# Gate matmuls and selection transposes on another pair of PSUM banks, and 12 expert dot products from one stage to the next

## The chip, the cores and the metric

One Trainium2 chip, one of its cores. The metric is the device time of one execution in microseconds (us). Engines are named as in the profile: PE is the matmul engine (TensorE), PEld its weight loads, which run beside the matmuls, DVE is VectorE, ACT is ScalarE, POOL is GpSimd, SP is the engine that issues the plain DMAs.

## What is computed

A decoder trunk of two layers over 272 tokens (16 meta tokens and 256 of the sequence) of width 1024, all in float32. Each layer first mixes tokens (an RG-LRU group and a latent-attention group) and then adds a PEER block, which this change touches:

```
x += W_out [ norm(RG-LRU group) ; norm(MLA group) ]
h  = RMSNorm(x)
q  = (h @ wq) as (token, 8 heads, 2 halves, 128)
s  = q . subkeys                       # 128 scores for each half
top 16 of each half -> 256 pair sums -> top 16 experts of 128*128, gates = softmax
x += sum over the 8*16 experts:  gate * gelu(h . u[expert]) * v[expert]
```

So for each token 128 of 16384 experts count, and u and v are tables of 16384 rows of 1024 numbers, 64 MB each for one layer.

## The kernel before

**Dense and sparse tokens.** For most tokens (SD = 224 of the 256 in layer 0, 208 in layer 1) a layer is computed densely. The *u stage* runs over 128 blocks j of 128 experts: it loads the block of u (1024 x 128 numbers, 512 KB), multiplies it with all tokens, and puts gelu of the result into the large tile `act` (128 experts x 128 blocks x SD tokens). The *gates* multiply `act` by a matrix that is zero but for the 128 chosen experts of each token. The *v stage* runs over 128 blocks of v and adds v times `act` into four PSUM banks. The other 48 tokens (in layer 0 the 16 meta tokens and 32 more, in layer 1 the last 48) are computed sparsely, in three groups g of 16 tokens: a gather is one indirect DMA, issued by POOL, of 128 rows (16 tokens by 8 heads, the s-th of the 16 picks) from u or v. A gathered u tile gives dot products on DVE (`w = 0`, L1067), a gathered v tile is scaled and added on DVE (`w = 1`, L1069 and L1071). A layer has 3 x 2 x 16 = 96 gathers, and the 32 dots of the groups 0 and 1 may be done early, in the u stage; what is not done there is spread over the v stage.

**One order for all loads.** `order` is written out when the program is made: for each stage its blocks, and between them the gathers. `UB` says how many gathers are put between u blocks: an entry (lo, hi, n) spreads n of them over the blocks lo to hi. Layer 0 has 17 of them, so 79 fall into its v stage; layer 1 has 32, so 64 fall into its v stage, about one every second block (`VEND`). Loads are issued in that order, the plain ones by SP, the gathers by POOL, into a ring of 7 tiles of 512 KB (`raw`), which parts of `act` and `gtab` join when they are free; a load waits until its tile has been read. Loaded tiles are taken in the same order.

**Three matmuls for one.** A block is split into two float16 tiles, hi on ACT (L230) and lo on DVE (L231), in three buffers each (`NHL`), two blocks ahead of PE. A u block is 24 matmuls: 8 x (hi by hi, hi by lo: L256, L257) and 8 of lo (L260); a v block is 24 at L1165.

**Work between the u blocks.** `bgq` is a list of generators, one after another, and `pump`, called once for each u block, advances the first until the costs that it yields have used up a credit. Their order: the top-16 searches (`top_head`), `dense_sel(0)`, `dense_sel(1)`, then `gates`. `dense_sel(t)` picks the experts of 128 tokens on DVE (`select_idx`) and then, for two index tiles and the gate values, transposes on PE into a g bank (L940), which DVE copies to `gtab` (L943, L945, L946). `gates` goes in steps b of 8 tokens (28 in layer 0, 26 in layer 1): one-hot tiles on DVE and ACT (`onehot`, L967 to L974), two banks of 8 matmuls each (`mm`, L983), and then `act` times the bank on DVE for the blocks that are done (L993), and a copy of the bank on ACT for those that are not (L995).

**PSUM.** `ps(tag)` gives the next bank of a tag: u has 2 banks, g has 2, v has 4. Banks of a tag go round, and an instruction that writes one waits until its earlier content has been read. In the u stage the blocks use u; the transposes, the gates, and the row tiles of the sparse tokens (L1038) use g. The v banks hold the query matmuls before the u stage and the four sums of the v stage after it.

The program is ordered for each engine by a planner (Tile) that follows the order of the text, with its own estimate of when an instruction can start; each engine then runs its list in order.

Of the kernel before, what the change touches and what calls it, by code (L numbers as in the profile page):

```python
# [46 lines left out]
WS = 1024.0  # L47
NSP = (32, 48)
NU = (2, 2)
UB = (((64, 127, 16), (116, 124, 1)), ((60, 127, 32),))  # L50
PF = 7
XV = 6
NHL = 3
# [91 lines left out]
def trunk(tc, a, out, dbg=None):  # L145
# [6 lines left out]
    def bc(ap, axis, n):  # L152
        ap = ap.unsqueeze(axis)
        s = list(ap.shape)
        s[axis] = n
        return ap.to_broadcast(s)

    def flat(ap):
        return ap.rearrange("p a b -> p (a b)")

    with ExitStack() as ctx:
# [6 lines left out]
        def ps(tag):  # L168
            return psp.tile([128, 512], F32, name="ps_" + tag, tag=tag, bufs=PB[tag])

        def gathers(l):
            ng = (NM if l == 0 else 0) // 16 + NSP[l] // 16
            r = [(g, w) for g in range(ng) for w in range(2)]
            r = [(g, 0) for g in range(NU[l])] + [x for x in r if x[1] or x[0] >= NU[l]]
            return [(g, w, s) for g, w in r for s in range(16)]

        order = []
        for l in range(L):
# [4 lines left out]
            for b in range(NK):  # L183
                order.append(("uT", l, b))
                want = sum(n * min(max(b - lo, 0) / (hi - lo), 1.0) for lo, hi, n in UB[l])
                while len(gathers(l)) - len(gs) < want:
# [85 lines left out]
        def area(tag, dt, shape=None, name=None):  # L272
            return per.tile(shape or [128, 8, T], dt, name=name or tag, tag=tag)
# [561 lines left out]
        def peer(l, col, hh, hl, rs, wq0):  # L835
            with tc.tile_pool(name="peer", bufs=1) as pp:
# [64 lines left out]
                bgq = []  # L901
                credit = [0.0]

                def pump(budget):
                    credit[0] = min(credit[0] + budget, 2.0)
                    while credit[0] > 0 and bgq:
                        try:
                            credit[0] -= next(bgq[0])
                        except StopIteration:
                            bgq.pop(0)  # L910

# [11 lines left out]
                def dense_sel(t):  # L923
                    r = {}
                    c0 = cur[0]
                    yield from select_idx(al, tv[t], ti[t], 8, GSCALE, r)
                    cur[0] = c0
                    if t == 1 and SD < S:
                        if l:
                            V.tensor_scalar(out=comb[:, 1], in0=flat(r["ix"][:, 1]), scalar1=128.0 * l, scalar2=None, op0=ALU.add)  # L930
                        V.scalar_tensor_tensor(out=comb[:, 0].bitcast(I32), in0=comb[:, 1] if l else flat(r["ix"][:, 1]), scalar=128.0, in1=flat(r["ix"][:, 0]), op0=ALU.mult, op1=ALU.add)
                        A.activation(comb[:, 1], flat(r["ga"]), AF.Copy, scale=1.0 / GSCALE)
                        for g in range(n0g // 16, NG):
                            p = toks[g] - NM - 128
                            ready.add(g)
                            for h in range(8):
                                G.dma_start(out=egs[h * 16:h * 16 + 16, g], in_=comb[p:p + 16, :, h * 16:h * 16 + 16])  # L937
                    for k, srct in enumerate((r["ix"][:, 0], r["ix"][:, 1], r["ga"])):
                        tp = ps("g")
                        P.transpose(tp[:, 0:128], flat(srct), ident)  # L940
                        s = slice(t * 128, t * 128 + 128)
                        if k < 2:
                            V.tensor_copy((i1T, i2T)[k][:, s], bc(tp[:, 0:128], 2, 2))  # L943
                        else:
                            V.tensor_copy(gh[:, s], bc(tp[:, 0:128], 2, 2))  # L945
                            V.tensor_tensor(out=gl[:, s], in0=tp[:, 0:128], in1=gh[:, s, 0], op=ALU.subtract)  # L946
                        yield 0.3
# [4 lines left out]
                def gates():  # L952
                    for e in range(NK * SD + 2 * D + 512, PS - D, D):
                        free.append((st["conv"] - 1, l, flata[:, e:e + D]))
                    oh["a"] = area("gx", F16, [128, 2, 2, 8, 128], "oha")
                    oh["b"] = area("gy", F16, [128, 2, 2, 8, 128], "ohb")
                    NB = SD // 8
                    iob = bc(iota, 1, 8)

                    def pairs(ap):  # L960
                        return ap.rearrange("p t (j e) -> p t j e", e=2)

                    def onehot(b):
                        s = slice(b * 8, b * 8 + 8)
                        oa, oe = oh["a"][:, b % 2, 0], oh["a"][:, b % 2, 1]
                        ob = oh["b"][:, b % 2]
                        V.tensor_tensor(out=pairs(oa), in0=iob, in1=bc(i1T[:, s], 2, 64), op=ALU.is_equal)  # L967
                        yield 0.6
                        V.tensor_tensor(out=pairs(oe), in0=iob, in1=bc(i2T[:, s], 2, 64), op=ALU.is_equal)  # L969
                        yield 0.6  # L970
                        V.tensor_tensor(out=pairs(ob[:, 0]), in0=pairs(oe), in1=bc(gh[:, s], 2, 64), op=ALU.mult)
                        yield 0.6
                        for t in range(8):
                            A.activation(ob[:, 1, t], oe[:, t], AF.Copy, scale=gl[:, b * 8 + t:b * 8 + t + 1])  # L974

                    def mm(b):
                        oa, ob = oh["a"][:, b % 2, 0], oh["b"][:, b % 2]
                        r = []
                        for s in range(2):
                            g = ps("g")  # L980
                            for t in range(4):
                                for k in range(2):
                                    P.matmul(g[:, t * 128:t * 128 + 128], oa[:, s * 4 + t], ob[:, k, s * 4 + t], start=t == 0 and k == 0, stop=t == 3 and k == 1, skip_group_check=True)  # L983
                            r.append(g)
                        return r

                    def mult(b, gs):
                        J = prog["u"]
                        for s, g in enumerate(gs):
                            t0 = b * 8 + s * 4  # L990
                            gv = g.rearrange("p (t j) -> p j t", t=4)
                            av = act[:, 0:J, t0:t0 + 4]
                            V.scalar_tensor_tensor(out=av, in0=av, scalar=1.0 / GSCALE, in1=gv[:, 0:J], op0=ALU.mult, op1=ALU.mult)  # L993
                            if J < NK:
                                A.activation(act[:, J:NK, t0:t0 + 4], gv[:, J:NK], AF.Copy, scale=1.0 / GSCALE)  # L995
                        prog["t"] = (b + 1) * 8
                        yield 0.14 + J * 8 / 960.0

                    for b in range(NB + 1):
                        if b < NB:  # L1000
                            yield from onehot(b)
                        if b:
                            gs = mm(b - 1)
                            yield from mult(b - 1, gs)
# [114 lines left out]
                if l == 0:  # L1119
                    bgq.append(sparse_top())  # L1120
                bgq += [dense_sel(0), dense_sel(1), gates()]
                xh, xlo = hnh[:, :, NM:NM + SD], hnl[:, :, NM:NM + SD]
                gt2 = pp.tile([128, 2, SD], F32, name="gt2")

                for j in range(NK):
                    w = block("uT", l, j)
                    if j % 2 == 0:
                        o2 = ps("u")
                    mm3(o2[:, (j % 2) * SD:(j % 2) * SD + SD], w, xh, xlo, first=j % 2 == 0)
                    if j % 2:  # L1130
                        td = prog["t"]
                        ov = o2[:, 0:2 * SD].rearrange("p (j t) -> p j t", j=2)
                        if td < SD:
                            A.activation(act[:, j - 1:j + 1, td:SD], ov[:, :, td:SD], AF.Gelu, scale=1.0 / WS)  # L1134
                        if td:
                            A.activation(gt2[:, :, 0:td], ov[:, :, 0:td], AF.Gelu, scale=1.0 / WS)  # L1136
                            V.tensor_tensor(out=act[:, j - 1:j + 1, 0:td], in0=act[:, j - 1:j + 1, 0:td], in1=gt2[:, :, 0:td], op=ALU.mult)
                        prog["u"] = j + 1
                    pump(PUMP[1] - prog["t"] / 960.0)
# [91 lines left out]
```

## Time and profile before

| | us |
|---|---|
| median of 3 runs | 1651.68 |
| lowest and highest | 1649.93, 1652.34 |
| the profiled execution | 1654.24 |
| its span, from the first to the last instruction | 1652.5 |
| mean granted clock of PE | 0.991 |

The profile is of one execution. Busy times are of its span; the 1.7 us between span and time lie before the first and after the last instruction. A matmul's end is modelled, so a pause of PE is better read from its weight loads.

### The profile page before, as it was taken

To read this page: it belongs to the slowest core of one execution; us is meant where nothing else is said; L and a number is where in the kernel's file an instruction comes from. 1 tells how busy PE (TensorE), PEld (TensorE's weight loads), DVE (VectorE), ACT (ScalarE), POOL (GpSimd) and SP (SyncE) were. 2 spreads that over 40 slices of the span, in tenths; PEclk is the share of its full clock that TensorE was granted. 3 is DMA by queue.
4 is the path that set the end of the run, shared out by engine and by line. 5 is a ranking of instruction groups with operands and counts; after the bars stand their busy time and mean duration, and the time that the engine had idled before them with its cause. 6 is when DMAs were issued, how large, how long until landed. Compare 5 with 4: busy or idle time off the path is not lost. (4 is left out here: it accounts for less than half of the span.)

```text
span 1652.5 us, 40158 instructions
## 1 busy us (share of the span) xinstructions
PE 1581.6 (96%) x15926; PEld 1474.2 (89%) x15926; DVE 1503.8 (91%) x3074; ACT 1096.1 (66%) x2001; POOL 348.6 (21%) x256
## 2 busy tenths in 40 slices
PE   9999998999998999999999899889998999999998
PEld 6667898999998999999977678779998999999998
DVE  6889999979989999999978889998899999999996
ACT  6857565789886655555557665567988766555554
POOL 1000000101111434544310000002131144743240
PEclk9999999999999999999999999999999999999999
DMA  8304465667777999999963044568678899999993
GB/s 307 115 7 165 140 220 199 219 196 243 243 241 255 343 408 383 353 365 368 339 243 111 31 144 141 179 215 261 205 281 277 274 338 408 395 375 358 370 367 115
DMA packets 117709, 421.22 MB, mean 255 GB/s; under 512 B 14416, under 2 KB 15824, under 8 KB 117008
## 3 DMA queue, kind: packets, MB, share of 16 engines
q1 hardware_dynamic: 88592, 317.88, 53.9%
q0 software_dynamic: 28928, 100.76, 16.7%
q8 instruction: 125, 2.05, 0.5%
q14 instruction: 64, 0.52, 0.1%
HBM read 417.46 MB, written 1.05 MB: 253 GB/s over the span
## 5 line engine op out<-in xcount | busy, mean ns | idle before, releaser
L230 ACT ACTIVATE hi<-raw 128x1024 f16<-128x1024 f32 x450 | 473.3, 1054 | 259.9 <-PE ps_v L1165 114.9
L231 DVE SCALAR_TENSOR_TENSOR lo<-raw,hi 128x1024 f16<-128x1024 f32 x450 | 549.8, 1225 | 53.5 <-ACT hi L230 45.5
L1165 PE MATMUL ps_v<-ww,hi 128*128 128x224 f16 (+1 forms) x4096 | 422.2, 256 | 2.8 <-ACT ww L1146 1.7
L256 PE MATMUL ps_u<-hn,hi 128*128 128x224 f16 (+2 forms) x2112 | 417.2, 258 | 4.8 <-ACT act L1134 3.5
L257 PE MATMUL ps_u<-hn,hi 128*128 128x224 f16 (+2 forms) x2112 | 416.9, 258 | 0.0
L1165 PEld LDWEIGHTS <-hi 128*128 128x128 f16 x4096 | 380.4, 98 | 3.5 <-issue 3.5
L256 PEld LDWEIGHTS <-hi 128*128 128x128 f16 x2656 | 261.6, 98 | 21.4 <-issue 7.9
L257 PEld LDWEIGHTS <-hi 128*128 128x128 f16 x2656 | 261.3, 98 | 19.9 <-issue 8.6
L260 PEld LDWEIGHTS <-lo 128*128 128x128 f16 x2656 | 248.1, 98 | 31.6 <-DVE lo L231 20.7
L260 PE MATMUL ps_u<-hn,lo 128*128 128x224 f16 (+2 forms) x2112 | 242.9, 257 | 13.2 <-DVE lo L231 13.0
L1165 PE MATMUL ps_v<-ww,lo 128*128 128x224 f16 (+1 forms) x2048 | 233.6, 256 | 1.0 <-DVE lo L231 1.0
L230 ACT ACTIVATE hi<-act 128x1024 f16<-128x1024 f32 x122 | 128.9, 1057 | 113.8 <-PE ps_v L1165 93.9
L1165 PEld LDWEIGHTS <-lo 128*128 128x128 f16 x2048 | 190.8, 98 | 1.2 <-DVE lo L231 1.2
L1084 POOL DMA_INDIRECT raw<-ur,act x68 | 97.5, 1434 | 360.5 <-DVE lo L231 206.5
L231 DVE SCALAR_TENSOR_TENSOR lo<-act,hi 128x1024 f16<-128x1024 f32 x122 | 148.9, 1224 | 17.0 <-ACT hi L230 15.7
L937 POOL DMA_DIRECT2D act<-act x40 | 20.3, 518 | 603.5 <-DMA raw<-uT 599.8
L974 ACT ACTIVATE ohb<-oha,gtab 128x128 f16<-128x128 f16 x432 | 137.0, 396 | 13.1 <-DVE oha L969 11.9
L256 PE MATMUL ps_v<-hgx,hi 128*128 128x272 f16 (+1 forms) x480 | 114.4, 278 | 2.7 <-DVE hT L1206 2.5
L257 PE MATMUL ps_v<-hgx,hi 128*128 128x272 f16 (+1 forms) x480 | 114.1, 278 | 0.2 <-DVE hgx L325 0.2
L1084 POOL DMA_INDIRECT raw<-v,act x46 | 79.6, 1731 | 96.9 <-DVE lo L231 79.8
L1084 POOL DMA_INDIRECT act<-v,act x43 | 76.7, 1785 | 89.5 <-DVE lo L231 70.8
L1147 DVE TENSOR_TENSOR ww<-act,ww 128x448 f16<-128x448 f32 (+1 forms) x128 | 77.1, 604 | 0.0
(321 smaller groups left out, 2009.7 us busy)
## 6 DMA issues: line engine op xcount, KB each, us to landing
raw<-uT SPq DMA_DIRECT2D x239, 512.0 KB
raw<-v SPq DMA_DIRECT2D x135, 512.0 KB
act<-v SPq DMA_DIRECT2D x105, 512.0 KB
raw<-wq SPq DMA_DIRECT2D x32, 512.0 KB
raw<-w_in SPq DMA_DIRECT2D x28, 512.0 KB
act<-uT SPq DMA_DIRECT2D x17, 512.0 KB
raw<-w_out SPq DMA_DIRECT2D x16, 512.0 KB
gtab<-v SPq DMA_DIRECT2D x16, 512.0 KB
```

Of the source, the lines that this page charges most:

```text
L230: A.activation(hi, r, AF.Copy, scale=WS)
L231: V.scalar_tensor_tensor(out=lo, in0=r, scalar=WS, in1=hi, op0=ALU.mult, op1=ALU.subtract)
L256: P.matmul(o, hi[:, s], xhi[:, c], start=first and c == 0, stop=False, skip_group_check=True)
L257: P.matmul(o, hi[:, s], xlo[:, c], start=False, stop=False, skip_group_check=True)
L260: P.matmul(o, lo[:, s], xhi[:, c], start=False, stop=c == n - 1, skip_group_check=True)
L937: G.dma_start(out=egs[h * 16:h * 16 + 16, g], in_=comb[p:p + 16, :, h * 16:h * 16 + 16])
L974: A.activation(ob[:, 1, t], oe[:, t], AF.Copy, scale=gl[:, b * 8 + t:b * 8 + t + 1])
L1084: G.indirect_dma_start(out=t, out_offset=None, in_=tab, in_offset=bass.IndirectOffsetOnAxis(ap=ei[g][:, s:s + 1], axis=0))
L1147: V.tensor_tensor(out=ww[:, b, 1], in0=act[:, j:j + 2], in1=ww[:, b, 0], op=ALU.subtract)
L1165: P.matmul(o, (hi, hi, lo)[k][:, s], (wh, wl, wh)[k], start=j == 0 and k == 0 and c % 2 == 0, stop=j == NK - 1 and k == 2, skip_group_chec ...
```

## The change

Four edits. In layer 1, 20 instead of 32 gathers stand between the u blocks 60 to 127, so that 12 dots, and their gathers, fall into the v stage, which then has 76. The three transposes of `dense_sel` and the two banks of a gate step are taken from tag v instead of g. Before its transposes `dense_sel` yields None, at which `pump` stops for this block, so that they come one u block later. NHL stays 3.

```diff
-UB = (((64, 127, 16), (116, 124, 1)), ((60, 127, 32),))
+UB = (((64, 127, 16), (116, 124, 1)), ((60, 127, 20),))
@@ pump
                         try:
-                            credit[0] -= next(bgq[0])
+                            c = next(bgq[0])
+                            if c is None:
+                                break
+                            credit[0] -= c
                         except StopIteration:
@@ dense_sel
+                    yield None
                     for k, srct in enumerate((r["ix"][:, 0], r["ix"][:, 1], r["ga"])):
-                        tp = ps("g")
+                        tp = ps("v")
                         P.transpose(tp[:, 0:128], flat(srct), ident)
@@ gates, mm
                         for s in range(2):
-                            g = ps("g")
+                            g = ps("v")
```

## Rows read from the trace of the kernel before

**Rows 1.** The first part of the page: busy time, share of the span and instructions of each engine.

```profile
PE 1581.6 (96%) x15926; PEld 1474.2 (89%) x15926; DVE 1503.8 (91%) x3074; ACT 1096.1 (66%) x2001; POOL 348.6 (21%) x256
```

**Rows 2.** Waits of the whole span: engine, what waited and at which line, for what, then us in total, times, longest us.

```profile
PEld L983 <- issue: 16.8, 17, 2.5
...
PEld ps_g L940 <- DVE gtab L943: 8.6, 2, 4.7
```

**Rows 3.** PE in order of time, rows around the selection and the gates of both layers: start us, us, line, operation, tiles, shapes, and in brackets the idle time before it and what ended it.

```profile
291.53 0.47 PE L940 MATMUL ps_g<-cst,act 128*128 128x128 f32 x1 [3.69 <-DVE gtab L943]
...
294.78 0.93 PE L260 MATMUL ps_u<-hn,lo 128*128 128x224 f16 x8
...
530.42 1.86 PE L983 MATMUL ps_g<-ohb,oha 128*128 128x128 f16 x16 [2.36 <-ACT act L995]
...
539.00 0.93 PE L260 MATMUL ps_u<-hn,lo 128*128 128x224 f16 x8
...
541.30 0.93 PE L260 MATMUL ps_u<-hn,lo 128*128 128x224 f16 x8
...
1111.12 0.47 PE L940 MATMUL ps_g<-cst,act 128*128 128x128 f32 x1 [4.45 <-DVE gtab L943]
...
1112.61 1.54 PE L260 MATMUL ps_u<-hn,lo 128*128 128x208 f16 x8
...
1280.98 0.82 PE L983 MATMUL ps_g<-ohb,oha 128*128 128x128 f16 x8 [2.06 <-ACT act L995]
```

**Rows 4.** Four short windows: the window and its length in us, busy us (and instructions) of each engine, the granted clock of PE as a share of its full speed, the share of the DMA engines, GB/s.

```profile
291.00:298.00 7.00, 6.47 (x51) 5.84 (x52) 7.00 (x17) 4.68 (x5) 0.00 (x0) 0.76 0.63 212
527.00:540.00 13.00, 10.64 (x103) 10.14 (x101) 10.95 (x15) 5.42 (x12) 2.80 (x3) 0.87 0.76 262
1111.00:1116.00 5.00, 4.88 (x39) 4.43 (x40) 3.96 (x10) 2.91 (x4) 0.00 (x0) 0.70 0.61 210
1280.00:1288.00 8.00, 7.02 (x67) 6.70 (x67) 8.00 (x13) 6.27 (x17) 2.07 (x2) 0.79 0.74 250
```

**Rows 5.** Waits in layer 1's v stage, from 1356 us to 1650, columns as in rows 2.

```profile
POOL act L1084 <- DVE lo L231: 60.6, 18, 11.9
...
DVE acc L1071 <- DMA raw<-v,act: 3.0, 2, 2.5
...
PEld L1165 <- DVE lo L231: 1.2, 1, 1.2
```

**Rows 6.** Windows by stage, columns as in rows 4, in the order PE, PEld, DVE, ACT, POOL: layer 0's gates, to the end of its u stage; layer 1's gates; layer 0's v stage; layer 1's v stage, then a stretch near its end and one around its beginning.

```profile
340.00:542.00 202.00, 195.71 (x2188) 192.75 (x2186) 185.64 (x276) 166.45 (x428) 30.47 (x21) 0.99 0.71 234
...
1186.00:1333.00 147.00, 137.22 (x1601) 133.49 (x1602) 143.96 (x221) 122.38 (x313) 36.51 (x25) 0.99 0.77 268
543.00:845.00 302.00, 300.31 (x3124) 299.88 (x3123) 278.21 (x339) 166.38 (x199) 125.27 (x84) 1.00 0.96 361
1366.00:1646.00 280.00, 278.36 (x3111) 277.96 (x3108) 254.85 (x275) 161.48 (x195) 111.43 (x59) 1.00 0.91 345
...
1620.00:1640.00 20.00, 20.00 (x224) 20.00 (x222) 16.34 (x17) 10.16 (x12) 0.00 (x0) 1.00 0.10 35
...
1356.00:1381.00 25.00, 23.52 (x263) 23.19 (x261) 24.92 (x31) 16.43 (x27) 13.66 (x6) 1.00 1.02 404
```

**Rows 7.** DVE in order of time, lo tiles after the two waits of the transposes: of the eight in layer 0 the first and the last, and two of layer 1.

```profile
288.42 1.23 DVE L231 SCALAR_TENSOR_TENSOR lo<-raw,hi 128x1024 f16<-128x1024 f32 x1
...
307.51 1.23 DVE L231 SCALAR_TENSOR_TENSOR lo<-raw,hi 128x1024 f16<-128x1024 f32 x1
...
1111.98 1.22 DVE L231 SCALAR_TENSOR_TENSOR lo<-raw,hi 128x1024 f16<-128x1024 f32 x1
1114.24 1.23 DVE L231 SCALAR_TENSOR_TENSOR lo<-raw,hi 128x1024 f16<-128x1024 f32 x1 [1.04 <-PE ps_u L260]
```

**Rows 8.** Waits in the gate stretches, columns as in rows 2: PEld in layer 0's (340 to 542), PEld in layer 1's (1186 to 1333), ACT in layer 0's.

```profile
PEld L983 <- issue: 5.4, 5, 2.5
...
PEld L983 <- issue: 11.4, 12, 2.2
...
ACT act L995 <- DVE act L993: 26.6, 18, 5.4
```

**Rows 9.** DVE in order of time in layer 1's gates: one dot and the lo tile after it.

```profile
1217.01 1.23 DVE L1067 SCALAR_TENSOR_TENSOR raw<-raw,act 128x1024 f32<-128x1024 f32 x1
...
1218.15 1.23 DVE L231 SCALAR_TENSOR_TENSOR lo<-raw,hi 128x1024 f16<-128x1024 f32 x1
```

**Rows 10.** Groups of DVE's instructions in layer 1's gates (1186 to 1333): count, busy us, mean ns of one, idle us before them. These are the early dots.

```profile
L1067 DVE SCALAR_TENSOR_TENSOR raw<-raw,act 128x1024 f32<-128x1024 f32 x20 | 24.4, 1222 | 1.9 <-ACT act L1039 1.9
...
L1067 DVE SCALAR_TENSOR_TENSOR act<-act 128x1024 f32<-128x1024 f32 x5 | 6.1, 1223 | 0.0
```

**Rows 11.** The gathers' line on POOL, first in layer 1's gates (1186 to 1333), then in its v stage (1356 to 1646): duration ns min/median/max, first and last start us.

```profile
L1084 POOL DMA_INDIRECT raw<-ur,act x20: 947/1688/1887, 1190.4 to 1327.2; - x20
...
L1084 POOL DMA_INDIRECT raw<-v,act x22: 947/1996/3667, 1360.6 to 1616.2; - x22
```

**Rows 12.** POOL in order of time, early in layer 1's v stage.

```profile
1407.29 3.66 POOL L1084 DMA_INDIRECT act<-v,act  x1 [0.30 <-issue]
1411.26 3.66 POOL L1084 DMA_INDIRECT raw<-v,act  x1 [0.30 <-issue]
```

**Rows 13.** The chain of work that ended last, a piece of it: start us, us, what. It is a gather from its issue to its landing.

```profile
1381.31 8.79 DMA raw<-v,act
```

## The prediction

> **What bounds the kernel now.** I read the page's head and busy line first, then the waits of TensorE, the clock, and the same stretches by engine. [rows 1]: PE is busy for 96% of the span and DVE for 91%, so most of the time is bare matmul time, and only what TensorE stands idle for can be won. [rows 2] names the idle time at the edited lines. Its weight-load rows are the truest, since matmul ends are modelled: 16.8 us in 17 waits before the gate matmuls (L983), and 8.6 us in 2 waits before the third selection transpose (L940), for DVE's copy of an earlier one (L943). [rows 3] shows the longest and what ended them: the transposes at 291.53 and 1111.12, and the gate matmuls at 530.42 and 1280.98, which waited for ACT's read-out of an earlier gate bank (L995). There are two g banks; a gate step takes both, and three transposes want three.
>
> **The clock after a long stop.** In [rows 4] the granted clock is 0.76, 0.87, 0.70 and 0.79 in four short windows, which lie on just these four stops of 2.06 us or more. The lower level is 1.2 GHz, half of the upper 2.4. The full-speed time lost in each is the window times what is missing: 7 x 0.24 = 1.7, 13 x 0.13 = 1.7, 5 x 0.30 = 1.5, 8 x 0.21 = 1.7, together 6.6 us. If the stops go, so do these.
>
> **The ceiling.** 16.8 + 8.6 + 6.6 + 1.2 (one wait for a lo tile early in layer 1's v stage, [rows 5]) = 33.2 us. The edit touches no other TensorE wait.
>
> **What may hold the gain back** is DVE. [rows 6]: in layer 0's gate stretch (340 to 542) DVE is busy 185.6 of 202 us, so 16 are free; in layer 1's (1186 to 1333) 143.96 of 147. There TensorE's waits only mirror a full DVE: take the wait alone away, and TensorE waits next for the lo tiles that DVE makes.
>
> **Part 1, transposes on v banks and a block later.** No instruction is added. With four banks the third transpose no longer needs the first one's copy. The delay takes six transposes and their copies one block back (2.30 us in layer 0 by [rows 3], x 208/224 columns = 2.14 in layer 1), and the gates behind them. Their last matmuls are at 530.42 in layer 0, whose v stage begins at 543, and before 1333 in layer 1, with the v stage from 1366 [rows 3, 6]. Those 12 us or more hide it; past them, each block would cost its 2.3.
> What is late next is a lo. Layer 0: the eight lo tiles after the stop begin between 288.42 and 307.51 [rows 7], and the eighth is ready 1.2 later, at 308.7. Before, the lo matmuls of the first of these blocks began at 294.78 and, at 2.30 a block, those of the eighth at 294.78 + 7 x 2.30 = 310.9. So 2.2 comes back by then unless DVE is relieved too; the ends are 2.2 and 3.7 + 1.7 = 5.4, and I take 2.5, near the row. Layer 1: the lo of 1111.98 is ready at 1113.2 [rows 7], and TensorE reached its block, two after that of 1112.61, at 1112.61 + 2 x 2.14 + 0.6 of half clock (eight lo matmuls took 1.54 there, 0.93 at 541.30 with more columns, [rows 3]) = 1117.5. DVE had caught up by then: at 1114.24 it waited 1.04 for TensorE [rows 7]. So 4.3 comes back (ends 2.2 as in layer 0, and 4.5 + 1.5 = 6.0).
>
> **Part 2, gates on four v banks.** Step b now needs the bank of step b-2, not of b-1. A step takes (530.42 - 340)/27 = 7.1 us in layer 0 [rows 3, 6] and the longest wait was 2.5 [rows 2], so the bank itself should never bind again. The v banks are idle here: the last query matmul is past, and the sums of the v stage want them only after the last gate read-out. Layer 0: 5.4 us of waits [rows 8] + 1.7 of clock = 7.1 at most, 0 at least. ACT stands 26.6 us behind DVE's multiply in this stretch [rows 8], and hi casts queue behind that read-out, so a part turns up again as a late hi or lo; DVE has 16 us free, and I take 5. Layer 1: 11.4 [rows 8] + 1.7 = 13.1 at most, which needs part 3.
>
> **Part 3, 12 dots from u to v.** A dot holds DVE for 1.14 us from its start to the next instruction's ([rows 9], 1217.01 to 1218.15; the accumulator read lies under it). Layer 1's gate stretch holds 20 + 5 = 25 of the 32 dots [rows 10]. 20/32 of them, 15.6, stay, and DVE gets 9.4 x 1.14 = 10.7 us lighter: 133.2. TensorE without its waits needs 147 - 13.1 = 133.9. At the 98% that DVE shows before, it takes 136, a gain of 11; two engines equally full jostle, so 10 (ends 3.0, DVE's idle time with nothing moved, and 13.1).
> In v, 12 x 1.14 = 13.7 us come on top of DVE's 254.9 of 280 [rows 6]: 96%. That costs 0, if all of it falls into the 25 us that DVE idles there, and 13.7 if none does. The nearest row is layer 0's v stage: 79 gathers against the 76 here, DVE at 92%, 361 GB/s, and TensorE's weight loads idle for 2.1 us in all [rows 6]. I take 1.5. The transfers: 12 x 0.524 MB = 6.3 MB more, 15.6 us at the 404 GB/s of full queues at 1356; the engines are all but empty (0.10) in the 20 us from 1620 [rows 6], so it fits. The early wait for a lo [rows 5] came with DVE 3.0 us behind late gathers; DVE enters v less behind, so 1.0 of the 1.2 comes back. On POOL the 12 issues move behind the other early ones, and only DVE's dots wait for them; SP's loads draw on the same buffers, which u gets back and v gives.
> The Trainium skill, "SBUF — State Buffer", section "SBUF: two separate sides", says that the descriptors of POOL-queue DMAs can't be written while DVE runs a two-port fast mode. DVE makes its float16 one-hot tiles in u alone, so by that rule gathers issue faster in v and the moved ones cost nothing: the sum would be 1.5 us better. The trace does not agree: an issue takes 1688 ns in the middle in u and 1996 in v [rows 11].
>
> **Sum.** 2.5 + 4.3 + 5 + 10 + 1.0 - 1.5 = 21.3 us. The profiled execution took 1654.24 us (span 1652.5, 1.7 around it): 1632.9. It lay 2.56 above the median of the runs, so 1630.4; I say **1630 us**.
>
> **Rivals.**
> *The wait moves* (0.22). The gate matmuls run ahead, and TensorE then waits for hi and lo: layer 0's gates give nothing, layer 1's half. For it: DVE at 98%, ACT 26.6 us behind DVE. Against: 12 dots leave. 2.5 + 4.3 + 0 + 5 + 1 - 1.5 = 11.3: 1640.
> *DVE's work is only moved* (0.07), so the change does not do what it is to do. If DVE bounds layer 1 from the selection to the end, its 4.3 is not had, and u's 10.7 comes back as 13.7 in v: 2.5 + 10.7 - 13.7 = -0.5, so 1652, no change that can be measured. For it: DVE's 143.96 of 147 us; against: its 25 idle us in v.
> *Gathers pace layer 1's v stage* (0.07; slower). From 1407 on each issue took 3.67 us on POOL and came 3.97 after the one before [rows 12]. If all 76 ran so, the stage takes 76 x 3.97 + 8.8 for a landing [rows 13] = 311 against 280: 31 lost, 1661. It decides from a spacing of (280 + 21 - 8.8)/76 = 3.85 us. Against: layer 0 brought 79 in 302 us, 3.82 each, and POOL itself mostly waits in v for a tile to be read, 60.6 us for those in act alone [rows 5].
> The skill's "DMA: Bandwidth & Descriptors", section "SWDGE vs HWDGE vs iDMA", says that the software and hardware queues take turns in each DMA engine. Half of 404 GB/s would be 2.6 us a gather, 197 us for 76: by that rule this rival can't decide. At 3.97 us the row gives gathers a third of the rate, less than that.
> *All of it* (0.05). The whole ceiling: 1654.2 - 33.2 - 2.6 = 1618.
>
> **How the numbers follow.** The forecast has 0.59, its own range 1622 to 1638. With *the wait moves*, out to 1645, the range **1620 to 1645** holds 0.81. About 0.2% (3.3 us) is what a measurement here can tell. Faster 0.86 (forecast, moved wait, all of it), same 0.07, slower 0.07.
>
> **What would show it.** Right: no L940 waiting for L943 and no L983 waiting for L995 among TensorE's waits; no clock dip near 290, 530, 1110, 1280; 28 rather than 16 gathers from ur in layer 1's v stage, DVE near 96% there. Wrong: as much new waiting of L256, L257 or L260 in u for hi or lo tiles (the wait moved), or of L1165 for lo tiles while DVE waits for gathers (paced by gathers).

## The result and the profile after

The changed kernel takes **1637.68 us** (median of 4 runs, 1636.75 to 1638.29) against 1651.26 for the kernel before on the same chip: a ratio of 0.9918, 95% interval 0.9900 to 0.9935, so 13.6 us or 0.8% less. The forecast was 1630 with 1620 to 1645. The time lies in the range, and just inside the forecast's own (1622 to 1638), but 7.7 us above the forecast and nearer to the rival *the wait moves* (1640). The profiled execution took 1637.41 us, its span 1635.6. From L908 on, lines of the changed file are three higher, and four from the transposes on: these are L944, the gate matmuls L987, their read-outs L997 and L999, the dots L1071, gathers L1088, the gelu read-out of a u bank L1138, v matmuls L1169.

The first part of the page after, which answers [rows 1] (busy time, share of the span and instructions of each engine):

```profile
PE 1574.9 (96%) x15926; PEld 1469.6 (90%) x15926; DVE 1501.4 (92%) x3073; ACT 1092.9 (67%) x2000; POOL 336.8 (21%) x256
```

The span fell by 16.9 us. TensorE runs the same 15926 matmuls, and DVE is busy for 2.4 us less: what went is idle time, and matmuls at half clock.

Waits of the whole span, the kernel before and then after (engine, what waited, for what, then us in total, times, longest us). Of after there is no row left for the gate matmuls or the third transpose, which made 16.8 and 8.6 us in [rows 2]:

```profile
PEld L260 <- DVE lo L231: 20.7, 31, 1.9
...
PEld L257 <- issue: 8.6, 15, 1.1
...
PEld L256 <- ACT hi L230: 2.1, 4, 0.9
```

```profile
PEld L260 <- DVE lo L231: 28.1, 42, 3.9
...
PEld L257 <- issue: 13.9, 22, 1.8
...
PEld L256 <- ACT hi L230: 7.0, 11, 1.2
```

25.4 us of waits left, and 7.4 + 5.3 + 4.9 = 17.6 us came in at the u blocks' own matmuls, for lo tiles, hi tiles and what stands behind them.

Short windows of after at the places of [rows 4], and a new one, 492 to 502 (window and length, busy us and instructions of PE, PEld, DVE, ACT, POOL, granted clock, DMA share, GB/s):

```profile
286.00:293.00 7.00, 6.15 (x62) 5.48 (x60) 6.93 (x22) 4.68 (x5) 0.00 (x0) 1.00 0.64 213
492.00:502.00 10.00, 6.33 (x56) 5.60 (x54) 7.27 (x11) 4.05 (x11) 2.69 (x2) 0.83 0.50 185
524.00:537.00 13.00, 12.85 (x141) 12.68 (x139) 12.31 (x17) 7.55 (x15) 4.55 (x3) 1.00 0.76 272
1108.00:1113.00 5.00, 5.00 (x59) 5.00 (x57) 5.00 (x9) 4.80 (x7) 0.00 (x0) 1.00 0.65 188
1273.00:1281.00 8.00, 7.44 (x89) 7.09 (x88) 8.00 (x12) 6.06 (x18) 1.69 (x1) 1.00 0.76 274
```

All four dips of the clock are gone, as forecast, and one has come where there was none (before, the clock is 1.00 in 494 to 503, round the same blocks). The stages of [rows 6], after: layer 0's gates, layer 1's gates (1178.6 to 1316.6, between the same blocks as 1186 to 1333 before), layer 0's v stage, layer 1's v stage, same columns:

```profile
340.00:536.00 196.00, 191.86 (x2154) 189.93 (x2152) 180.53 (x269) 162.90 (x419) 25.30 (x20) 0.99 0.70 234
1178.60:1316.60 138.00, 134.82 (x1601) 131.32 (x1600) 133.92 (x202) 118.99 (x310) 21.55 (x15) 1.00 0.74 257
537.00:840.00 303.00, 300.04 (x3123) 299.87 (x3123) 279.52 (x337) 166.46 (x200) 126.18 (x85) 1.00 0.96 363
1352.00:1631.00 279.00, 278.59 (x3114) 278.33 (x3111) 265.32 (x303) 160.11 (x192) 122.93 (x70) 1.00 0.93 363
```

Layer 1's v stage carries 12 more dots (DVE 265 of 279 us, 95%) and TensorE is busy for 278.6 of 279.

Stretches that begin and end at other times are compared by blocks. This table, worked out from the traces, is the time from the first lo matmul (L260) of one u block to that of another, and for the v stage from the end of its first lo matmuls to its last matmul ("to v": from block 127's first lo matmul to that end). The kernels are those of the experiments below. Each column is one execution. Kernels with the same layer 0 (after, e4 and e8; e1 and e9) differ by up to 0.8 us in its u rows and 1.2 in its v stage, so less than that in one row is read only where several kernels repeat it.

```
us                 before  e1    e2    e3    e4    e9    e10  after  e6    e8    e11
L0 u 34-44           29.0  29.1  29.1  28.7  28.7  29.1  28.7  28.7  28.7  28.7  28.5
L0 u 56-100         122.1 120.1 122.5 124.2 120.1 120.1 124.1 120.5 120.1 120.1 120.1
L0 u 100-127         77.2  75.7  77.2  75.7  74.8  75.8  75.5  75.6  70.1  75.6  70.1
L0 to v               5.2   7.0   5.2   5.2   6.9   7.4   5.2   6.9   5.2   7.4   5.2
L0 v                297.6 297.6 297.6 297.6 297.6 298.8 297.6 297.6 300.9 298.8 300.3
L1 u 26-44           46.1  47.6  46.3  43.5  43.5  46.9  43.5  43.5  43.5  43.5  42.9
L1 u 58-112         151.4 151.0 146.9 151.8 151.5 141.3 146.8 142.3 142.3 137.6 141.3
L1 u 112-127         32.1  32.1  32.1  32.1  32.1  32.9  32.1  32.9  32.9  32.1  32.9
L1 v                278.5 278.2 277.3 278.1 278.3 277.3 277.3 277.3 277.3 289.1 277.3
span               1652.5 1650.2 1646.0 1647.9 1644.8 1638.9 1640.0 1635.6 1632.3 1643.0 1628.3
```

### The profile page after: what moved, and what is told of

Read it like the earlier page. It is cut to its first block, busy times and chain, and to the rows that moved or that the text cites. A ratio compares the mean times of both kernels' runs of the same rounds, so it can differ in the third digit from the quotient of the medians.

```text
span 1635.6 us, 40192 instructions
## 1 busy us (share of the span) xinstructions
PE 1574.9 (96%) x15926; PEld 1469.6 (90%) x15926; DVE 1501.4 (92%) x3073; ACT 1092.9 (67%) x2000; POOL 336.8 (21%) x256
## 5 line engine op out<-in xcount | busy, mean ns | idle before, releaser
L230 ACT ACTIVATE hi<-raw 128x1024 f16<-128x1024 f32 x442 | 463.8, 1055 | 236.5 <-PE ps_v L1169 111.9
L231 DVE SCALAR_TENSOR_TENSOR lo<-raw,hi 128x1024 f16<-128x1024 f32 x442 | 536.1, 1217 | 44.0 <-ACT hi L230 40.3
L1169 PE MATMUL ps_v<-ww,hi 128*128 128x224 f16 (+1 forms) x4096 | 422.3, 256 | 4.5 <-DVE ww L1151 2.8
L1169 PEld LDWEIGHTS <-hi 128*128 128x128 f16 x4096 | 380.4, 98 | 5.2 <-issue 5.2
L257 PEld LDWEIGHTS <-hi 128*128 128x128 f16 x2656 | 260.4, 98 | 24.6 <-issue 13.9
L260 PEld LDWEIGHTS <-lo 128*128 128x128 f16 x2656 | 246.5, 98 | 38.7 <-DVE lo L231 28.1
L260 PE MATMUL ps_u<-hn,lo 128*128 128x224 f16 (+2 forms) x2112 | 242.2, 257 | 18.0 <-DVE lo L231 17.5
L1169 PE MATMUL ps_v<-ww,lo 128*128 128x224 f16 (+1 forms) x2048 | 233.5, 256 | 0.0
L1169 PEld LDWEIGHTS <-lo 128*128 128x128 f16 x2048 | 190.9, 98 | 0.0
L1088 POOL DMA_INDIRECT raw<-ur,act x69 | 93.2, 1351 | 374.3 <-DVE lo L231 224.4
L1088 POOL DMA_INDIRECT act<-v,act x44 | 86.5, 1967 | 71.1 <-DVE lo L231 41.1
L1088 POOL DMA_INDIRECT raw<-v,act x49 | 72.9, 1488 | 97.0 <-DVE lo L231 48.6
```

What stands on the lines that cost most here:

```text
L230: A.activation(hi, r, AF.Copy, scale=WS)
L231: V.scalar_tensor_tensor(out=lo, in0=r, scalar=WS, in1=hi, op0=ALU.mult, op1=ALU.subtract)
L257: P.matmul(o, hi[:, s], xlo[:, c], start=False, stop=False, skip_group_check=True)
L260: P.matmul(o, lo[:, s], xhi[:, c], start=False, stop=c == n - 1, skip_group_check=True)
L1088: G.indirect_dma_start(out=t, out_offset=None, in_=tab, in_offset=bass.IndirectOffsetOnAxis(ap=ei[g][:, s:s + 1], axis=0))
L1169: P.matmul(o, (hi, hi, lo)[k][:, s], (wh, wl, wh)[k], start=j == 0 and k == 0 and c % 2 == 0, stop=j == NK - 1 and k == 2, skip_group_chec ...
```

## The experiments

The question was which edit earns what. The theory: in layer 1's gates two limits stand in series, the two g banks and a full DVE, and each hides the other. Its rivals: DVE alone is the limit (the moved dots are all of the gain), or the banks alone are. Kernels of one wave were compared with runs of the kernel before on the same chip, whose medians were 1652.0 (e1 to e4), 1652.4 (e5 to e8) and 1653.66 (e9 to e12).

**e1_gates_v: the banks alone** (on the kernel before)

```diff
                         for s in range(2):
-                            g = ps("g")
+                            g = ps("v")
```

> The kernel before with one edit: the gate banks on tag v. Theory A (two limits in series: in layer 1's gates DVE is full, 143.96 of 147 us, so banks alone give at most its 3 us of idle time there, and about 1.4 in layer 0): about 1647 us, the L983 waits for L995 gone, new waits of L260 for lo tiles in layer 1 of about 8 us. Rival B (only DVE's work counts): 1651, nothing. Rival C (only the banks count): 8.2 in layer 1 and 1.4 in layer 0 as in the changed kernel, 1642.

Measured: 1653.24, ratio 1.0010 [1.0002, 1.0019]. Weight-load waits of layer 1's gates (1180 to 1333), and the stretch as a window:

```profile
PEld L257 <- issue: 3.6, 3, 1.7
PEld L260 <- DVE lo L231: 2.6, 5, 0.6
PEld L983 <- issue: 2.5, 5, 1.6
PEld L256 <- ACT hi L230: 1.4, 2, 0.7
```

```profile
1186.00:1333.00 147.00, 138.30 (x1611) 133.85 (x1610) 145.29 (x222) 122.03 (x309) 38.84 (x26) 0.99 0.77 271
```

The wait for the bank fell from the 11.4 us of [rows 8] to 2.5, and 3.6 + 2.6 + 1.4 us of other waits stand in its place; DVE is busy for 145.3 of 147 us, and the blocks take 151.0 instead of 151.4. More banks alone buy nothing where the engine that reads and feeds them is full. The theory's time, 1647, was missed by 6 us: by the time alone the rival that only DVE's work counts (1651) is nearer, and e9 decides against it. In layer 0, where DVE has idle time, the blocks 56 to 127 win 2.0 + 1.5 us and 1.8 is given back on the way to v. The Trainium skill, "Perfetto Trace Analysis", section "Matmul Optimizations", asks for all 8 PSUM banks to be used; in the u stage this run puts work on the four that lay idle, and it is no faster.

**e2_dots: the dots alone**

```diff
-UB = (((64, 127, 16), (116, 124, 1)), ((60, 127, 32),))
+UB = (((64, 127, 16), (116, 124, 1)), ((60, 127, 20),))
```

> The kernel before with one edit: 20 early dots in layer 1 instead of 32. Theory A: DVE is 10.7 us lighter in layer 1's gates, but the read-outs still hold the two g banks; about half of the 11.4 us of L983 waits goes, and 1 us at the start of v: 1645. Rival B (only DVE's work counts): all of layer 1's 8.2 and the 1.3 of v, 1642. Rival C: only the 1.3 of v, 1650. If the 12 dots cost in v what they hold DVE there (13.7 us), slower than 1651 in B's or C's case.

Measured: 1647.43, ratio 0.9969 [0.9959, 0.9979]. The window of layer 1's gates, and what TensorE waits for there (1180 to 1330):

```profile
1185.00:1327.00 142.00, 135.19 (x1593) 132.61 (x1593) 137.11 (x207) 120.89 (x314) 21.89 (x15) 0.99 0.76 258
```

```profile
PEld L983 <- issue: 7.6, 8, 3.0
```

Now DVE has 5 us to spare and the banks hold TensorE for 7.6. The blocks gain 4.5 us, and layer 1's v stage does not get longer with its 12 dots: 277.3 instead of 278.5. The time lies between the theory's 1645 and the 1650 of the rival that only the banks count.

**e3_sel: the selection's edits alone** (its transposes on v, and the block's delay)

```diff
+                    yield None
                     for k, srct in enumerate((r["ix"][:, 0], r["ix"][:, 1], r["ga"])):
-                        tp = ps("g")
+                        tp = ps("v")
```

> The kernel before with two edits: selection transposes on tag v and a block later. Theory A: the 8.6 us of waits and two clock dips go, most comes back as waits for lo and hi while DVE is full with the selection: 0.4 us in layer 0 and 2.6 in layer 1, 1648. Rival D (TensorE that runs ahead meets the full DVE of layer 1's gates and loses its 2.6 there): 1651. If my first working held: 2.5 + 4.3, 1644.

Measured: 1649.26, ratio 0.9985 [0.9975, 0.9995]. Blocks 34 to 44 of layer 0 win 0.3 us, blocks 26 to 44 of layer 1 win 2.6; further on layer 0 loses 2.1 (blocks 56 to 100) and wins 1.5 (100 to 127). That loss comes with the gates on g alone: e10 has it too, the kernels with the gates on v don't.

**e4_no_dots: all but the dots** (the changed kernel)

```diff
-UB = (((64, 127, 16), (116, 124, 1)), ((60, 127, 20),))
+UB = (((64, 127, 16), (116, 124, 1)), ((60, 127, 32),))
```

> The changed kernel with 32 early dots again in layer 1. Theory A: of layer 1's 8.2 us some 3 stay (DVE's idle time), and the wait for late gathers at the start of v comes back, 1.3: 1644. Rival B: all 8.2 and 1.3 are lost, 1647. Rival C: only the 1.3 of v is lost, 1639.

Measured: 1650.72 (1645.89 to 1653.46), ratio 0.9989 [0.9980, 0.9998]; its profiled execution is one of its short ones, 1646.67. Layer 1's gates are where they were (151.5): banks without DVE's relief bring nothing there with the selection's edits either. The theory had 3 us of gain there and 1644, and missed by 6.7; where the other executions lost 4 us against the profiled one, no trace shows.

**e9_dots_gates: dots and banks, the selection as before**; **e10_dots_sel: dots and selection, gates on g.** Their diffs are those of e1 and e2, and of e3 and e2, together.

> The kernel before with the gate banks on v and with 12 dots moved to layer 1's v stage, but the selection's transposes on g as before. Theory (two limits in series: the g banks and DVE, each hides the other): layer 1's gate stretch (u blocks 58 to 112, 151.4 us before) falls by about 8 us to 143, though banks alone gave 0.4 there and dots alone 4.5; the transposes' wait of 8.6 us at L940 stays; with the 1 to 1.3 us that a shorter run-up of gathers gives layer 1's v stage and about 1.5 us in layer 0's gates the time is near 1640.5 (1638 to 1642.5). Rival (the selection's edits are the other half of the pair, because they let the gates start earlier): banks and dots only add up, 0.4 + 4.5 in that stretch, and the time is near 1648, that of the dots alone.

> The kernel before with 12 dots moved to layer 1's v stage and the selection's edits, gates still on g. Theory (banks and DVE in series): layer 1's gate stretch falls only by the 4.5 us that the dots alone gave, to 147, with about 12 us of waits at the gate matmuls left; the transposes give 0.4 us in layer 0 and 2.6 in layer 1, as the selection's edits alone did; the time is near 1645 (1643 to 1647). Rival (the selection's edits are the other half of the pair): the stretch falls to 143 or below and the time to 1640 or less.

Measured: e9 1641.88, ratio 0.9932 [0.9920, 0.9945]; e10 1643.04, 0.9940 [0.9928, 0.9952]. e9's layer 1 gates as a window, then the waits there of e10 (1180 to 1325):

```profile
1180.00:1316.00 136.00, 133.32 (x1592) 129.95 (x1590) 133.01 (x202) 119.26 (x312) 23.02 (x16) 1.00 0.73 251
```

```profile
PEld L987 <- issue: 6.9, 8, 1.5
```

This is the pair. Blocks 58 to 112 win 0.4 us by the banks alone, 4.5 by the dots alone, and 10.1 by both (e9), with the selection untouched; with the selection's edits in place of the banks (e10) they win 4.6, the dots' share, and the bank's wait stays. (e10's time came out at the low end of what was expected.) Two limits in series are shown; that either alone is the limit, and that the selection's edits are half of the pair, fall.

**e5_no_delay: the changed kernel without the block's delay**

```diff
-                    yield None
```

> The changed kernel without the block's delay of the transposes. If the four banks alone took the transposes' waits away: 1638, as the changed kernel. If TensorE now waits for DVE's index tiles in the middle of a block, each of the four first transposes late by a block's share: 2 to 4 us more, 1640 to 1642.

Measured: 1636.73, ratio 0.9909 [0.9896, 0.9922], which overlaps the changed kernel's interval by most of its length. The delay is worth nothing that can be measured: with a bank for each transpose none waits, whether it comes early or late. By blocks it even costs: without it layer 1's blocks 26 to 44 take 42.9 instead of 43.5 us, and its blocks 58 to 112 take 141.3 instead of 142.3, as in e9 and e11, which have no delay either.

**e6_l0_8: the changed kernel with layer 0's early dots spread otherwise.** The profile after has one long stop, at 493. Its rows, in order of time, of POOL, DVE and PE after (start us, us, line, what, in brackets the idle time before it and what ended it):

```profile
487.69 2.73 POOL L1088 DMA_INDIRECT raw<-ur,act  x1 [10.61 <-DVE lo L231]
...
494.73 1.23 DVE L1071 SCALAR_TENSOR_TENSOR raw<-raw,act 128x1024 f32<-128x1024 f32 x1 [5.13 <-DMA raw<-ur,act]
...
497.15 0.94 PE L260 MATMUL ps_u<-hn,lo 128*128 128x224 f16 x8 [3.67 <-DVE lo L231]
```

And DVE and PEld of the kernel before at the same place:

```profile
496.71 1.23 DVE L1067 SCALAR_TENSOR_TENSOR raw<-raw,act 128x1024 f32<-128x1024 f32 x1 [5.54 <-DMA raw<-ur,act]
...
499.13 0.69 PEld L260 LDWEIGHTS <-lo 128*128 128x128 f16 x8 [1.69 <-DVE lo L231]
```

A gather got its buffer late and was issued at 487.69; DVE, which runs its list in order, stood 5.13 us before the dot that needs it, with the lo tile that TensorE needed next queued behind it. The stall is an old one (5.54 us before). There TensorE, still behind from its bank waits, met 1.69 us of it; after, it had caught up and met 3.67 and a dip of the clock. The edit takes gathers away from there:

```diff
-UB = (((64, 127, 16), (116, 124, 1)), ((60, 127, 20),))
+UB = (((64, 127, 8),), ((60, 127, 20),))
```

> The changed kernel with 8 instead of 17 early dots in layer 0, so 88 gathers in its v stage. Theory E (layer 0's gates gave little because a gather that lands late holds DVE for 5.1 us at 490, TensorE for 3.8 and its clock for 1.7, and because DVE enters v behind, 1.8): with half of these gathers gone and DVE 10 us lighter, 3 to 6 us less, 1632 to 1635. Rival F (layer 0's gates are held by ACT, which stands behind DVE's multiply): no more than 1 us, 1637. Rival G (layer 0's v stage cannot take 9 more, DVE 290 of 303): slower, up to 10 us.

Measured: 1634.38, ratio 0.9892 [0.9878, 0.9907]. DVE's only waits between 440 and 536, and the window that had the dip:

```profile
DVE lo L231 <- ACT hi L230: 7.5, 13, 1.2
```

```profile
492.00:502.00 10.00, 10.00 (x113) 10.00 (x112) 10.00 (x14) 7.66 (x18) 1.00 (x1) 1.00 0.69 227
```

No wait for a gather, TensorE busy for 10 of 10 us at the full clock. Layer 0 wins 5.5 us in blocks 100 to 127 and 1.7 on the way to v, and its v stage pays 3.3 for nine more dots. The 3.9 us of the stop and 10 x 0.17 = 1.7 of clock are most of these 7.2. The edit also takes some 10 us of dots (9 x 1.14) off DVE, and no run separates the two; the 1.7 on the way to v may be its part.

**e7_l0_0: no early dots in layer 0 at all**

```diff
-UB = (((64, 127, 16), (116, 124, 1)), ((60, 127, 20),))
+UB = ((), ((60, 127, 20),))
```

> The changed kernel with no early dot in layer 0, 96 gathers in its v stage, DVE about 299 of 303 us there and the transfers at 387 GB/s. Theory E: the u stage of layer 0 loses its last waits for gathers, 5 to 7 us; v gives back 0 to 5: 1631 to 1638. Rival G: v becomes bound by DVE or by gathers, slower than the changed kernel by 3 us or more.

Measured: 1638.44, ratio 0.9919 [0.9906, 0.9932]. The u stage wins 7.7 us by blocks, but layer 0's v stage takes 306.2 instead of 297.6 us and gives it all back, more than the 0 to 5 us expected.

**e8_l1_8: 24 instead of 12 dots moved in layer 1**

```diff
-UB = (((64, 127, 16), (116, 124, 1)), ((60, 127, 20),))
+UB = (((64, 127, 16), (116, 124, 1)), ((60, 127, 8),))
```

> The changed kernel with 8 instead of 20 early dots in layer 1, 88 gathers in its v stage. DVE in its gates gets about 11 us lighter, in v 13.7 us heavier, 279 of 279. If v hides dots as long as DVE has idle time and no longer: u gains what waits are left in its gates, some 5 us, v loses 3 to 8: 1636 to 1642. If v hides them wholly: 1633. If gathers pace v: slower than 1645.

Measured: 1645.20, ratio 0.9958 [0.9944, 0.9971]. The gates win another 4.7 us, and v loses 11.8. Its weight-load waits in v (L1049 is a matmul that sums the picks of a sparse group), and two windows with dips of the clock:

```profile
PEld L1169 <- DVE lo L231: 4.9, 14, 0.7
PEld ps_g L1049 <- issue: 4.4, 2, 2.9
```

```profile
1472.00:1479.00 7.00, 6.76 (x54) 6.27 (x55) 6.34 (x9) 2.07 (x3) 5.72 (x3) 0.76 1.02 408
1625.00:1633.00 8.00, 6.86 (x55) 6.53 (x56) 3.64 (x4) 1.06 (x1) 0.00 (x0) 0.79 0.00 0
```

4.9 + 4.4 of waits and 7 x 0.24 + 8 x 0.21 = 3.4 of clock make 12.7, about the 11.8: the dots' hiding place is full between 12 and 24. The loss was expected at 3 to 8, and a time above 1645 if gathers paced the stage; they hardly do, for in the whole stage DVE waits 1.8 + 0.9 us for gathers.

**e11_best: e5 and e6 together; e12_best16: with 16 instead of 12 dots moved**

```diff
-UB = (((64, 127, 16), (116, 124, 1)), ((60, 127, 20),))
+UB = (((64, 127, 8),), ((60, 127, 20),))
...
-                    yield None
```

In e12 layer 1's entry is (60, 127, 16).

> The changed kernel without the yield None and with layer 0's early dots spread otherwise (8 over the blocks 64 to 127, none bunched over 116 to 124). If the two steps are independent, the 1 us that leaving out the delay gave (1636.7 against 1637.7, about the size of the interval) and the 3.3 us of the other spread add up: 1633.5 (1632 to 1635.5), below both kernels. If the delay's microsecond was noise: 1634.4, as with the spread alone.

> As the run before it in this list, but with 16 instead of 20 early dots in layer 1, so 16 instead of 12 moved. Layer 1's gate stretch gave 9.1 us for 12 moved dots and 13.8 for 24, its v stage nothing for 12 and -11.8 us for 24. If v hides dots as long as DVE has idle time there (5% of 279 us = 14 us at 12, a dot takes 1.14, so some 12 more at the very most), four more cost v at most 2 us and the gates give 1.5 to 2: 1633 to 1634, no difference from the run before. If v starts to pay at once, at the rate of the 24 (1 us a dot): 1637. If v pays only past 16: 1632.

Measured: e11 1632.94 (1630.08 to 1633.78), ratio 0.9875 [0.9861, 0.9890]; e12 1632.28, ratio 0.9876 [0.9860, 0.9892]. Both beat both kernels, 1.2% below the one before, and can't be told from each other: with 16 dots moved, layer 1's v stage still takes 277.3 us, and its blocks 58 to 112 take 140.4 instead of 141.3. Layer 1's gates and v stage of e11:

```profile
1180.00:1315.00 135.00, 132.35 (x1577) 129.76 (x1575) 132.96 (x200) 115.67 (x294) 21.30 (x15) 1.00 0.77 260
1345.00:1624.00 279.00, 278.27 (x3110) 278.01 (x3108) 265.33 (x302) 159.81 (x190) 123.15 (x70) 1.00 0.93 363
```

## Why the prediction was right, and where it was 8 us off

What was right: the bound (idle time of TensorE, not work), the waits that vanish, the four clock dips, that the banks need DVE relieved, and the sign. The sum forecast 21.3 us; the medians differ by 13.6, and the table gives 0.3 + 2.6 + 1.5 + 8.3 + 1.2 = 13.9 for the same terms. The profiled execution of before was a long one, as allowed for: 2.3 us of the two spans' difference lie before the first u block, where nothing was changed. That the time came nearer to *the wait moves* is luck: that rival has 6.8 us for the transposes, of which 2.9 were measured, and 5 for layer 1's gates, which gave 8.3; the two errors cancel.

- **Layer-0 transposes, 2.5: measured 0.3.** The step "what is late next is a lo" was wrong: of what TensorE waited for, most was ACT's. Weight-load waits around the transposes, before (284 to 312) and then after (282 to 310):

```profile
PEld ps_g L940 <- DVE gtab L943: 3.9, 1, 3.9
PEld L260 <- DVE lo L231: 0.9, 2, 0.6
```

```profile
PEld L257 <- issue: 2.1, 2, 1.8
PEld L260 <- DVE lo L231: 2.0, 5, 0.7
PEld L256 <- ACT hi L230: 1.7, 3, 1.1
```

Of the 3.9 + 1.7 (clock) saved, 5.8 - 0.9 = 4.9 came back, 1.1 of it behind lo tiles. That leaves 0.7, or 0.3 by blocks. The longest of the new stops, PE and ACT after in order of time, and the window around it:

```profile
285.37 0.49 PE L944 MATMUL ps_v<-cst,act 128*128 128x128 f32 x3
...
304.41 0.26 PE L256 MATMUL ps_u<-hn,hi 128*128 128x224 f16 x1 [1.94 <-ACT act L1138]
```

```profile
297.08 1.91 ACT L812 ACTIVATE act<-act 128x2048 f16<-128x2048 f16 x1 [3.15 <-DVE act L815]
...
299.96 1.28 ACT L826 ACT_TABLE_LOAD   x1
301.25 0.31 ACT L826 ACTIVATE act<-act 128x128 f32<-128x128 f32 x1
301.47 1.04 ACT L230 ACTIVATE hi<-raw 128x1024 f16<-128x1024 f32 x1
302.52 1.28 ACT L1138 ACT_TABLE_LOAD   x1
303.82 0.54 ACT L1138 ACTIVATE act<-ps_u 128x448 f32<-128x448 f32 x1
```

```profile
300.00:308.00 8.00, 6.06 (x62) 5.89 (x63) 8.00 (x11) 7.96 (x13) 0.00 (x0) 1.00 0.56 187
```

  The three transposes now run together, and some blocks later TensorE stands 1.94 us until ACT has read out a u bank (L1138). ACT had loaded the table for a selection's exponential (L826), cast one hi, and loaded the table for gelu again, 1.28 us each load, and is busy for 7.96 of 8 us. But it entered that stretch late: the selection's own copy on ACT (L812), which stands in front in ACT's list, had waited 3.15 us for DVE (L815), against 0.48 before. So DVE, busy for 27.93 of the 28 us from 282 to 310, holds TensorE here too, by way of ACT. Before, TensorE was late anyway and no such wait shows. I had looked only at the lo tiles' times in [rows 7]. Neither moving the exponential nor moving L812 was tried, so how much each would win back stays open. The Trainium skill, "ScalarE: Activation LUTs", section "What ACT_TABLE_LOAD costs", has 1283 ns for a load, as here, and 1380 ns more for a drain; here a load begins 0.01 us after the cast and the next activation 0.02 us after the load, so the trace shows no such drain.
- **Layer-1 transposes, 4.3: measured 2.6.** Right in kind. The wait of 4.7 us and 1.5 of clock went, and of the weight-load waits round these blocks (before 1099 to 1146, after 1094 to 1139) those for lo grew by 1.3, those for hi by 1.4, and 0.9 came in behind them: 3.6 came back, where the forecast, 4.3 of 6.0, left 1.7 for that. The row varies, though: in e1, e2 and e9, which select as before, it is 46.3 to 47.6, so the term is 2.6 to 4.1.
- **Layer-0 gates, 5: measured 1.5.** u blocks 56 to 127 win 1.6 + 1.6, and 1.7 of it is given back on the way to v. The term's 7.1 us at most (5.4 of waits, 1.7 of clock) did go. What came back: TensorE, ahead now, met 3.92 instead of 1.69 us of DVE's wait for a late gather (+2.2), with a dip of the clock (+1.7), and it reached the v stage before the float16 split of `act` (`ww`) that its first matmuls read was ready (+1.7), which makes 1.5. The waits at the first v matmul, before (537 to 549) and after (533 to 545):

```profile
PE ps_v L1165 <- DVE ww L1147: 0.5, 1, 0.5
```

```profile
PE ps_v L1169 <- DVE ww L1151: 2.2, 1, 2.2
```

  "DVE has 16 us free" was the step that failed: 5.5 of the 16 were that one wait, during which DVE, which runs in order, could serve nobody. Without the stall (e6) the three rows are 120.1 + 70.1 + 5.2 = 195.4 against 204.5, 9.1 us, of which its v stage gives 3.3 back.
- **Layer-1 gates, 10: measured 9.1** by block 112, 0.8 of it lost by block 127, so 8.3. The working held: DVE 143.96 of 147 in [rows 6] became 133.92 of 138 (I had 133.2 of 136), and *the wait moves* gave 5.
- **The v stage, -0.5 in all: measured +1.2.** The early wait for a lo went, 1.2 of 1.2, and the 12 dots cost nothing at 95% of DVE; my 1.5 for them, taken from layer 0's v stage, was too high, and e12 shows 16 to be as free.
- **The rivals.** *The wait moves* was right for layer 0 (its 0 against 1.5 measured), wrong for layer 1 (its 5 against 8.3). *DVE's work is only moved* falls by e2 (4.5 us in u, no loss in v). *Gathers pace layer 1's v stage* falls: 76 gathers in 277.3 us are 3.65 us apart, below the 3.85 from which it decides, and no TensorE wait for a lo is left there. The rule of the Trainium skill that the prediction weighed ("SBUF — State Buffer", section "SBUF: two separate sides") had [rows 11] against it, but I misread them: they set gathers from ur in u against gathers from v in v. Like with like, ur into raw tiles, before already had 947 ns in the middle in v against 1688 in u, and after has 1058 against 1688, the way the rule would have it; ur into act tiles shows 1951 in v against 1688 in u before. That the one-hot tiles run in such a mode is shown by no row either, so the rows neither bear the rule out nor refute it, and the sum did not need it. The gathers' line, before in v (1356 to 1646), then after in u (1180 to 1316) and in v (1352 to 1631):

```profile
L1084 POOL DMA_INDIRECT raw<-ur,act x7: 947/947/1999, 1481.8 to 1547.7; - x7
```

```profile
L1088 POOL DMA_INDIRECT raw<-ur,act x11: 947/1688/1702, 1197.4 to 1311.5; - x11
```

```profile
L1088 POOL DMA_INDIRECT raw<-ur,act x12: 950/1058/2186, 1356.3 to 1542.0; - x12
```

## What to carry to other kernels

A wait that ends with a buffer's release is worth its length only if whoever feeds and empties the buffer has time to spare, so take the wait and the load away together, and time each alone: here they are worth 0.4 and 4.5 us apart and 10.1 together. Before crediting a wait, look for the other stalls nearby (a late gather in front of an in-order engine, a table load), since they are what the faster engine meets next. Work that was moved into another stage cost nothing here while it fitted well into that stage's idle time, and much once it filled it: at 1.14 us each, 12 and 16 dots are 13.7 and 18.2 of the 25 us that DVE idled there and cost nothing; 24 are 27.4 and cost 11.8.

## What the runs showed of the hardware

- The clock falls also after a stop that is no bank wait: after the 3.67 us for a lo tile the granted clock is 0.83 in 492 to 502, between its levels of 2.4 and 1.2 GHz; where the stall is gone (e6), 1.00. After the new stop of 1.94 us at 304 it stayed at 1.00.
- Two ACT table loads of 1.28 us each stood among the work that kept ACT from a u bank and stopped TensorE for 1.94 us, after a wait of 3.15 us for DVE, in a stretch (282 to 310) where ACT is busy for only 19.44 of 28 us.
